# The keys and values of layer 1's memory, computed behind those of layer 0

## The chip, the cores and the metric

The kernel runs on one core of a Trainium2 chip. The metric is device time in microseconds (us), median of several runs. The engines are PE (TensorE: matmuls and transposes, with PEld for its weight loads), DVE (VectorE), ACT (ScalarE), POOL (GpSimd) and SP (SyncE, which issues all DMAs, in order). Each engine carries out its instructions in the order in which the program has them.

## The reference

A trunk of two layers on x (512 x 1024, f32) with a memory of 256 rows. Layer 0 mixes with NSA attention, layer 1 with DSA attention; each layer also has four memory heads, an output projection and a SwiGLU feed-forward network. Cut to what matters here:

```python
for i in range(DEPTH):                                   # 2 layers
    xn = rmsnorm(h, norm_mix[i])
    mix, q_mem = nsa_mixer(xn, nsa_w_in, ...) if i == 0 else dsa_mixer(xn, ...)
    q_mem = q_mem.reshape(B, T, 4, 64) * 64 ** -0.5
    mem_o = memory_attention(q_mem, rmsnorm(mem, norm_mem[i]), w_mem_kv[i])
    h = h + jnp.concatenate([mix, mem_o], axis=-1) @ w_out[i]
    hn = rmsnorm(h, norm_ffn[i])
    h = h + (silu(hn @ ffn_gate[i]) * (hn @ ffn_up[i])) @ ffn_down[i]

def memory_attention(q_mem, mem_n, w_mem_kv):            # mem_n 256 x 1024, w_mem_kv 1024 x 512
    kv = (mem_n @ w_mem_kv).reshape(B, 256, 2, 4, 64)
    k, v = kv[:, :, 0], kv[:, :, 1]
    p = jax.nn.softmax(einsum('bthd,bmhd->bhtm', q_mem, k))
    return einsum('bhtm,bmhd->bthd', p, v)
```

`mem` is an input: its keys and values for layer 1 depend on nothing that layer 0 computes. All attention logits of the mixers get a relative-position bias, which depends on `rel_bias` alone.

## The kernel before

Every f32 product is done as three matmuls of halves: an operand is split into a high part (a cast by ACT) and a low part (the difference, by DVE, or by POOL with `split_ap`). A weight so goes DMA -> `raw` -> `whi` (ACT) -> `wlo` (DVE or POOL) -> PE. `proj_T` takes 128 columns of a weight (512 KB) at a time and has 24 matmuls for them; `proj_tok` takes 4 of the 8 row blocks at a time (512 KB).

A scheduler orders the instructions of each engine by their place in the source, by what they wait for and by when a tile's buffers come free; tiles of one tag share `bufs` buffers.

The start (L855-L878): the two row tiles of mem are loaded, scaled (`scale_row`, L238 on DVE), transposed (`to_T`, L252); `mem_kv` of layer 0 computes keys (`proj_T`, 48 matmuls of 256 columns) and values (`proj_tok`, 48); its four weights use the raw tiles that the projections use too (2 buffers). The four row tiles of x are scaled, both halves by POOL (XSP = (1,1): L235 times rstd, L236 times gain), and transposed. `build_rows` (L353-L377) makes the bias rows: a small matmul (o<-bk,rb, L369), a copy to `row` (L372), a DMA to DRAM `relrow`, and one DMA from `relrow` to `relskew`, which writes for each of 12 heads 128 shifted rows of 512 floats (3 MB). A head's rows come back from there as an M tile (L380, 256 KB, 2 buffers); POOL copies four pieces of each into C (L1038). Then follow the projections of x for layer 0 (nsa weights, matmuls of 512 columns, 24 for a load), the memory's attention (scores s<-kmh,qm at L470, softmax, transposes t<-ident,msb at L425, products), and the heads.

FFN0 (L776, `ffn(0, ...)`) runs eleven units c of gate and up projections with the down projection of the units before in between; FFN1 is the same code for layer 1. In FFN0 at c == 2 `other()` calls `mem_kv1` (L1261): mem is loaded again, its squares are summed again, and `mem_kv(1, ...)` makes the 16 transposes, 48 K matmuls and 48 V matmuls of layer 1's memory. The V weights are split by ACT and POOL (MWK[1] = (0,1)), the K weights by ACT and DVE. Results go to DRAM (`kvd`), from where layer 1 reads them.

## Time and profile before

| | |
|---|---|
| median of 3 runs | 1295.7 us (1294.3 to 1297.49) |
| the profiled execution | 1301.25 us, its span 1299.5 us |
| instructions in the span | 20995 |
| busy | PE 94%, DVE 74%, ACT 52%, POOL 22% |
| DMA | 127.02 MB, mean 98 GB/s |

The span is the stretch between the first and the last instruction in the trace. The page has each engine's busy time, the costliest groups of lines, and the DMA issues. The trace behind it gives, for one engine, a timeline with the idle time before each instruction and what ended it; windows with busy times, granted PE clock and DMA rate; and for a line or a tile its first and last instruction. A matmul's printed duration overlaps the next one's; the step from start to start is what one costs. Regions: the start to some 145 us, layer 0's attention, FFN0 from about 340 to 690 us, layer 1, FFN1 from about 940 to the end.

### The profile page before, as it was taken

The numbers are of one execution on the slowest core, as the hardware profiler recorded it, in microseconds if no ns is written. First come the engines' busy times: TensorE is split into PE (matmuls) and PEld (weight loads), VectorE is DVE, ScalarE is ACT, GpSimd is POOL, SyncE is SP. The second block draws the span as 40 slices with busy tenths as digits, with TensorE's granted clock in tenths as the row PEclk, the third lists the DMA queues.
The fourth block names the chain that finished last, engine by engine and source line by source line (L and its number), as shares of the span: only waits on it lengthen the run. The fifth ranks groups of instructions, "written<-read, shape, count | busy, mean of one in ns | idle before, by whom it ended". The sixth has DMA issues, their size and how long they took to land. (4 is left out here: it accounts for less than half of the span.)

```text
span 1299.5 us, 20995 instructions
## 1 busy us (share of the span) xinstructions
PE 1219.0 (94%) x7810; PEld 1079.4 (83%) x7810; DVE 967.7 (74%) x1763; ACT 672.4 (52%) x1370; POOL 284.6 (22%) x442
## 2 busy tenths in 40 slices
PE   5889999999898999999999778899999999999997
PEld 5668888888888999999998665667799999999995
DVE  6567568998976778777756789948987877777754
ACT  6357376596645444444444365456755444444442
POOL 6440246453301000000004036535420000000001
PEclk9989899999899999999999799999989999999999
DMA  6744221112355333333122010213425333333211
GB/s 228 212 151 118 78 61 51 49 58 71 93 170 180 105 114 98 98 98 111 53 91 81 26 65 29 69 56 110 127 85 154 117 108 107 98 98 98 66 66 65
DMA packets 154842, 127.02 MB, mean 98 GB/s; under 512 B 7240, under 2 KB 129128, under 8 KB 154740
## 3 DMA queue, kind: packets, MB, share of 16 engines
q1 hardware_dynamic: 154740, 125.68, 31.5%
q8 instruction: 61, 1.00, 0.3%
q14 instruction: 41, 0.34, 0.1%
HBM read 122.22 MB, written 6.58 MB: 99 GB/s over the span
## 5 line engine op out<-in xcount | busy, mean ns | idle before, releaser
L245 ACT CAST whi<-rq 128x1024 fp32r<-128x1024 f32 x128 | 134.3, 1051 | 212.2 <-issue 121.7
L246 DVE TENSOR_TENSOR wlo<-rq,whi 128x1024 fp32r<-128x1024 f32 x128 | 159.1, 1251 | 39.9 <-ACT whi L245 39.8
L214 POOL TENSOR_SCALAR ss<-ss 128x1 f32<-128x1 f32 x16 | 7.3, 455 | 627.8 <-ACT sq L212 627.8
L302 PE MATMUL s<-dlo,hh 128*128 128x512 f32 x320 | 125.9, 393 | 1.0 <-DVE dlo L246 1.0
L303 PE MATMUL s<-Xfl,hh 128*128 128x512 f32 x320 | 126.3, 395 | 0.0
L301 PE MATMUL s<-Xfl,hh 128*128 128x512 f32 x320 | 124.4, 394 | 0.0
L554 POOL TENSOR_SCALAR sb<-sb,sm 128x128 f32<-128x128 f32 (+3 forms) x144 | 76.7, 550 | 97.4 <-DVE sm L1384 45.7
L550 ACT ACTIVATE sb<-sb,mx 128x128 f32<-128x128 f32 (+3 forms) x144 | 79.5, 554 | 33.4 <-DVE mx L547 32.7
L688 PE MATMUL X<-Xxl,whi 128*128 128x256 f32 x320 | 89.6, 280 | 0.0
L690 PE MATMUL X<-Xxl,wlo 128*128 128x256 f32 x320 | 89.6, 280 | 0.0
L689 PE MATMUL X<-Xxl,whi 128*128 128x256 f32 x320 | 89.5, 280 | 0.0
L772 DVE TENSOR_TENSOR res<-s,res 128x512 f32<-128x512 f32 x96 | 65.6, 686 | 20.4 <-PE s L303 20.3
L544 DVE CUSTOM_DVE_ANT_0 sb<-s,M 128x512 f32<-128x512 f32 (+3 forms) x144 | 66.2, 482 | 16.6 <-PE s L537 5.6
L303 PEld LDWEIGHTS s<-Xfl,hh 128*128 128x128 f32 x320 | 60.0, 188 | 13.3
L302 PEld LDWEIGHTS s<-dlo,hh 128*128 128x128 f32 x320 | 60.1, 188 | 12.4 <-DVE dlo L246 1.3
L301 PEld LDWEIGHTS s<-Xfl,hh 128*128 128x128 f32 x320 | 60.0, 188 | 11.0 <-DVE res L772 0.3
L245 ACT CAST hh<-c 128x256 fp32r<-128x256 f32 x88 | 35.5, 405 | 56.2 <-DVE c L698 49.5
L689 PEld LDWEIGHTS X<-Xxl,whi 128*128 128x128 f32 x320 | 60.1, 188 | 1.8
L688 PEld LDWEIGHTS X<-Xxl,whi 128*128 128x128 f32 x320 | 60.2, 188 | 1.7
L690 PE MATMUL X<-Xfh,wlo 128*128 128x256 f32 x208 | 59.4, 286 | 2.0 <-DVE wlo L246 2.0
L245 ACT CAST pth<-t 128x512 fp32r<-128x512 f32 (+1 forms) x98 | 48.9, 521 | 23.5 <-PE t L425 20.3
L246 DVE TENSOR_TENSOR ptl<-t,pth 128x512 fp32r<-128x512 f32 (+1 forms) x98 | 57.5, 602 | 4.7 <-ACT pth L245 3.8
(474 smaller groups left out, 4128.7 us busy)
## 6 DMA issues: line engine op xcount, KB each, us to landing
rq<-in_ffn_gate_dram SPq DMA_DIRECT2D x88, 256.0 KB, 2.9
rq<-in_ffn_up_dram SPq DMA_DIRECT2D x88, 256.0 KB, 3.3
draw<-in_ffn_down_dram SPq DMA_DIRECT2D x20, 1024.0 KB, 4.9
M<-relskew SPq DMA_DIRECT2D x36, 256.0 KB, 2.7
raw<-in_w_out_dram SPq DMA_DIRECT2D x16, 512.0 KB, 3.6
raw<-in_nsa_w_in_dram SPq DMA_DIRECT2D x12, 512.0 KB, 4.4
relskew<-relrow SPq DMA_DIRECT2D x1, 3072.0 KB
raw<-in_w_mem_kv_dram SPq DMA_DIRECT2D x4, 512.0 KB, 7.8
```

Source lines behind the costliest of these rows:

```text
L245: act.copy(hi, src)
L246: dve.tensor_sub(lo, src, f(hi))
L301: pe.matmul(o, ah, bh, start=start, stop=False)
L302: pe.matmul(o, ah, bl, start=False, stop=False)
L303: pe.matmul(o, al, bh, start=False, stop=stop)
L544: dve.tensor_tensor_reduce(E[j, br].rearrange("p (k n) -> p k n", n=128), sv[:, :, x, :], Mi.rearrange("p (k n) -> p k n", n=128), 1.0, -3 ...
L550: act.activation(E[j, br], E[j, br], AF.Exp, bias=mx[:, j, br:br + 1], accum_out=sm[:, j, br:br + 1])
L554: pool.tensor_scalar(E[j, br], E[j, br], fc[:, j, br:br + 1], 0.0, op0=OP.mult, op1=OP.add)
L688: pe.matmul(oc, a, xh[:, k], start=first and m == 0 and k == 0, stop=False, skip_group_check=True)
L689: pe.matmul(oc, a, xl[:, k], start=False, stop=False, skip_group_check=True)
L690: pe.matmul(oc, b, xh[:, k], start=False, stop=m == 1 and k == 3, skip_group_check=True)
L772: dve.tensor_add(res[t][:, cs], p, res[t][:, cs])
```

## The change

1. `mem_kv1` is gone from FFN0, with `Two`, `other`, `mt` and `inplace`. Right behind `build_rows` the same `mem_kv(1, ...)` is called with the mem tiles and rstd that layer 0 used; its transposed rows lie in the big tile "fl", the keys in two tiles of the start's pool, the values in the buffer that qs[3] takes later. The results are written to DRAM from there.
2. All weights of `mem_kv` have raw tiles of their own (tag "mraw", 3 buffers).
3. norm_mix's gain has its own tag "gx".
4. XSP = (0,1): the first half of each x row is scaled by one instruction on DVE, the second by POOL as before.
5. In FFN0's tail two tiles are borrowed from other tags.

The diff, without the class `Two`, which is only removed:

```diff
@@ -29,6 +29,7 @@
 WBF = 3
 CHUNK = (2, 5, 3, 4)
 RQ = 6
+MRAW = 3
 WB1 = 2
 EH = 6
 WE = 6
@@ -59,7 +60,7 @@
 QMO = 0
 PT = ("st","t","","fst","o")
 MSP = ((0,0),(0,0))
-XSP = (1,1)
+XSP = (0,1)
 MWK = ((0,0),(0,1))
 PQE = (0,0,1,0,1,1)
 PRE_ = (0,0,0,1)
@@ -189,8 +179,8 @@
     def bcast_rows(src, n, dst):
         dma(dst, bass.AP(tensor=src.tensor, offset=src.offset, ap=[[0, dst.shape[0]], [1, n]]))
 
-    def gain(src, where, bufs=1):
-        g = where.tile([128, D], F32, name=nm("g"), tag="g", bufs=bufs)
+    def gain(src, where, tag="g"):
+        g = where.tile([128, D], F32, name=nm("g"), tag=tag, bufs=1)
         bcast_rows(src, D, g)
         return g
 
@@ -284,7 +274,8 @@
     def wraw(n, where=None):
         assert n <= 1024
         if where is not None:
-            return rq(where)
+            pool_, tag, bufs = where
+            return pool_.tile([128, 1024], F32, name=nm(tag), tag=tag, bufs=bufs)
         return WP["p"].tile([128, 1024], F32, name=nm("raw"), tag="raw", bufs=WP["r"])
 
     def rq(fp, dt=F32):
@@ -380,12 +371,12 @@
         dma(dst, skd[h, :, a:a + n])
 
 
-    def mem_kv(i, xm, rs, wk, kv, mt, f32=False, where=None, inplace=False):
+    def mem_kv(i, xm, rs, wk, kv, mt, f32=False, where=None):
 
         kmh, kml, vm = kv
         g = gain(A["norm_mem"][i], wk)
         for t in range(2):
-            xn = xm[t] if inplace else wk.tile([128, D], F32, name=nm("xn"), tag="xn", bufs=2)
+            xn = wk.tile([128, D], F32, name=nm("xn"), tag="xn", bufs=2)
             scale_row(xm[t], rs[t], g, xn, MSP[i])
             to_T(xn, mt[0], mt[1], t)
         W = A["w_mem_kv"][i]
@@ -782,7 +773,7 @@
             down_mm(t, half, ks, hh, hl, res)
             yield
 
-    def ffn(i, fp, gu0, X, res, fin, early=None, other=None, mt=None):
+    def ffn(i, fp, gu0, X, res, fin, early=None):
         parts = [(0, 1), (1, 3), (3, 5), (5, 7), (7, 9), (9, 11)]
         part_of = {c: pi for pi, (a, b) in enumerate(parts) for c in range(a, b)}
         hs = {}
@@ -793,8 +784,6 @@
                 drain(gu_plain(fp, R, X, *hs[c]))
                 X["sums"]()
                 continue
-            if c == 2 and other:
-                other()
             pi = part_of[c]
             a, b = parts[pi - 1] if pi > 1 else parts[0]
             half = c - parts[pi][0]
@@ -835,7 +824,7 @@
         phase(*PP0)
         W0 = A["nsa_w_in"][0]
         lp = L0.enter_context(_pool(tc, name="l0", bufs=1))
-        qs = {h: lp.tile([128, T], F32R, name=f"qs{h}") for h in range(4)}
+        qs = {h: lp.tile([128, T], F32R, name=f"qs{h}") for h in range(3)}
         mcat = [lp.tile([128, 2, T], F32R, name=f"mcat{x}") for x in range(2)]
         vc4 = lp.tile([128, 2, 4, 128], F32R, name="vc4")
         kcdh = lp.tile([128, 2, 32], F32R, name="kcdh")
@@ -865,8 +854,9 @@
                     rs.append(row_rstd(xm[t], scr))
                 slot = big.tile([128, 4096], F32R, name="mt0", tag="fh")
                 slot = slot.rearrange("p (a k q) -> p a k q", a=2, k=KD)
-                mem_kv(0, xm, rs, sp, kv0, [slot[:, a] for a in range(2)])
-                g = gain(A["norm_mix"][0], sp)
+                mw = (sp, "mraw", MRAW)
+                mem_kv(0, xm, rs, sp, kv0, [slot[:, a] for a in range(2)], where=mw)
+                g = gain(A["norm_mix"][0], sp, "gx")
                 for t in range(NT):
                     dma(res[t], A["x"][0, t * 128:(t + 1) * 128, :])
                 for t in range(NT):
@@ -874,6 +864,16 @@
                     scale_row(res[t], row_rstd(res[t], xn), g, xn, XSP)
                     to_T(xn, xh, xl, t)
                 build_rows(sp)
+
+                kp = [sp.tile([128, NMEM, MEML], F32R, name=f"km1{n}") for n in "ab"]
+                kp.append(lp.tile([128, 2, NMEM, 64], F32, name="vm1", tag="qs3"))
+                slot = big.tile([128, 4096], F32R, name="mt1", tag="fl")
+                slot = slot.rearrange("p (a k q) -> p a k q", a=2, k=KD)
+                mem_kv(1, xm, rs, sp, kp, [slot[:, a] for a in range(2)], True, mw)
+                for d, x in zip(kvd[:2], kp):
+                    dma(d, f(x.rearrange("p a b -> p (a b)")))
+                dma(kvd[2], kp[2].rearrange("p t h d -> p (t h d)"))
+            qs[3] = lp.tile([128, T], F32R, name="qs3", tag="qs3")
             mq = MA.enter_context(_pool(tc, name="mq", bufs=1))
             qm = [mq.tile([128, T], F32R, name=f"qm{h}") for h in range(NMEM)]
             ep = mq
@@ -1147,7 +1147,7 @@
 
         def fin():
             LA["x"] = [big.tile([128, KD, T], F32R, name=f"x1{n}", tag=n) for n in ("xh", "xl")]
-            nl = Lent(ng, dict(xn=(WP["h"], "wlo", 2), sq=(fp, "c12", 1)))
+            nl = Lent(ng, dict(xn=(fp, "hx", 2), sq=(fp, "c12", 1)))
             return norm_to(gain(A["norm_mix"][1], ng), *LA["x"], nl)
 
         def in_proj(fp):
@@ -1225,7 +1225,7 @@
                     if k0 + k < 6:
                         pair = [WP["p"].tile([128, 1024], F32R, name=nm(x), tag=x, bufs=WP["w"]) for x in ("whi", "wlo")]
                     else:
-                        pair = [WP["h"].tile([128, 1024], F32R, name=nm("w3"), tag="whi", bufs=2) for _ in range(2)]
+                        pair = [WP["h"].tile([128, 1024], F32R, name=nm("w3"), tag="raw", bufs=2) for _ in range(2)]
                     pair = [x[:, :912].rearrange("p (k c) -> p k c", c=456) for x in pair]
                     split(raw[:, k:k + 2, :], *pair)
                     ks += [(pair[0][:, j, :], pair[1][:, j, :]) for j in range(2)]
@@ -1258,21 +1258,7 @@
 
             return each
 
-        def mem_kv1():
-
-            kp = [ip.tile([128, NMEM, MEML], F32R, name=f"km1{n}", tag=n) for n in "ab"]
-            kp.append(ip.tile([128, 2, NMEM, 64], F32, name="vm1", tag="c"))
-            xm = [rq(fp) for _ in range(2)]
-            for t in range(2):
-                dma(xm[t], A["mem"][0, t * 128:(t + 1) * 128])
-            rs = [row_rstd(xm[t], fp.tile([128, 1024], F32, name=nm("S"), tag="S", bufs=1)) for t in range(2)]
-            mem_kv(1, xm, rs, ng, kp, mt, True, fp, True)
-            for d, x in zip(kvd[:2], kp):
-                dma(d, f(x.rearrange("p a b -> p (a b)")))
-            dma(kvd[2], kp[2].rearrange("p t h d -> p (t h d)"))
-
-        mt = [Two(*[hslot().rearrange("p (k q) -> p k q", k=4) for _ in range(2)]) for _ in range(2)]
-        ffn(0, fp, gu0, X, res, fin, in_proj, mem_kv1)
+        ffn(0, fp, gu0, X, res, fin, in_proj)
 
 
     with ExitStack() as L1:
```

Since the scheduler sets the order, here is what it made of it. SP's queue from the load of the bias rows on, before (raw_N: nsa weights; relrow, relskew: bias rows):

```order
L297 DMA raw_456<-in_nsa_w_in_dram 128x8x128
L373 DMA relrow<-row 12x640
L297 DMA raw_491<-in_nsa_w_in_dram 128x8x128
L377 DMA relskew<-relrow 1536x1x512
L297 DMA raw_526<-in_nsa_w_in_dram 128x8x128
L297 DMA raw_561<-in_nsa_w_in_dram 128x8x128
L884 DMA posrk<-in_nsa_cmp_pos_k_dram 16x128
L884 DMA posrv<-in_nsa_cmp_pos_v_dram 16x128
```

And after (mraw_N: weights of layer 1's memory, here both halves of the V weights; M_N: bias rows of one head):

```order
L364 DMA relrow<-row 12x640
L368 DMA relskew<-relrow 1536x1x512
L288 DMA mraw_547<-in_w_mem_kv_dram 128x4x256
L288 DMA mraw_553<-in_w_mem_kv_dram 128x4x256
L371 DMA M_1170<-relskew 128x512
L371 DMA M_1176<-relskew 128x512
L371 DMA M_1182<-relskew 128x512
L371 DMA M_1188<-relskew 128x512
L371 DMA M_1380<-relskew 128x512
L371 DMA M_1386<-relskew 128x512
L371 DMA M_1392<-relskew 128x512
L288 DMA raw_707<-in_nsa_w_in_dram 128x8x128
```

Behind relskew stood two loads of nsa weights; now the two V weight loads stand there, then seven M loads, and the third nsa load behind them.

POOL, before, from the last weight split ahead of the first C copies on (w2x: a weight of the compression):

```order
L258 TENSOR_TENSOR w2x_613<-w_76_610,w2x_612 128x256
L1038 TENSOR_SCALAR C<-M_989 128x31
L1038 TENSOR_SCALAR C<-M_989 128x23
L1038 TENSOR_SCALAR C<-M_989 128x15
L1038 TENSOR_SCALAR C<-M_989 128x7
L1038 TENSOR_SCALAR C<-M_995 128x31
L1038 TENSOR_SCALAR C<-M_995 128x23
```

POOL, after, between the two low halves of the V weights (wlo_550 from mraw_547, wlo_556 from mraw_553):

```order
L252 TENSOR_TENSOR wlo_550<-mraw_547,whi_549 128x1024
L1038 TENSOR_SCALAR C<-M_1170 128x31
L1038 TENSOR_SCALAR C<-M_1170 128x23
L1038 TENSOR_SCALAR C<-M_1170 128x15
L1038 TENSOR_SCALAR C<-M_1170 128x7
L1038 TENSOR_SCALAR C<-M_1176 128x31
```

and further on, up to the second of them:

```order
L1038 TENSOR_SCALAR C<-M_1182 128x31
L1038 TENSOR_SCALAR C<-M_1182 128x23
L1038 TENSOR_SCALAR C<-M_1182 128x15
L1038 TENSOR_SCALAR C<-M_1182 128x7
L252 TENSOR_TENSOR wlo_556<-mraw_553,whi_555 128x1024
L1038 TENSOR_SCALAR C<-M_1188 128x31
```

The low halves of the memory's V weights now stand on POOL, with the 12 copies of three M tiles between them.

PE, before, from the last V matmuls of layer 0's memory (f_280) to the first projection of x (f_462):

```order
L302 MATMUL f_280<-wlo_250,mt_126 128x256
L303 MATMUL f_280<-whi_249,mt_126 128x256
L252 MATMUL x_395<-ident,xn_385 128x128 x4
L252 MATMUL x_402<-ident,xn_385 128x128 x4
L301 MATMUL f_462<-xh_98,whi_458 128x512
L302 MATMUL f_462<-xl_99,whi_458 128x512
```

PE, after, in the V matmuls of layer 1's memory, at the first matmul that uses wlo_556 (f_559 and f_585: the two row tiles of mem):

```order
L293 MATMUL f_585<-wlo_550,mt_432 128x256
L294 MATMUL f_585<-whi_549,mt_432 128x256
L293 MATMUL f_559<-wlo_556,mt_432 128x256
L294 MATMUL f_559<-whi_555,mt_432 128x256
L292 MATMUL f_559<-whi_555,mt_432 128x256
```

and the end of these with the first projection (f_678):

```order
L292 MATMUL f_585<-whi_555,mt_432 128x256
L293 MATMUL f_585<-wlo_556,mt_432 128x256
L294 MATMUL f_585<-whi_555,mt_432 128x256
L292 MATMUL f_678<-xh_97,whi_674 128x512
L293 MATMUL f_678<-xl_98,whi_674 128x512
```

The projections of x now stand behind all of layer 1's K and V matmuls. At the memory's attention, before (f_738: a projection, s: scores, t: transposes of softmax rows msb):

```order
L302 MATMUL f_738<-xl_99,whi_734 128x512
L303 MATMUL f_738<-xh_98,wlo_735 128x512
L470 MATMUL s_772<-kmh,qm_440 128x256
L471 MATMUL s_772<-kml,qm_440 128x256
L470 MATMUL s_772<-kmh,qm_441 128x256
L471 MATMUL s_772<-kml,qm_441 128x256
L425 MATMUL t_697<-ident,msb_675 128x128
```

After (f_814: the fifth projection; no other one stands between these scores and their transposes):

```order
L294 MATMUL f_814<-xh_97,wlo_811 128x512
L461 MATMUL s_847<-kmh,qm_619 128x256
L462 MATMUL s_847<-kml,qm_619 128x256
L461 MATMUL s_847<-kmh,qm_620 128x256
L462 MATMUL s_847<-kml,qm_620 128x256
```

and, behind eight more score matmuls like these, PE goes straight to the transposes:

```order
L462 MATMUL s_953<-kml,qm_621 128x256
L461 MATMUL s_953<-kmh,qm_622 128x256
L462 MATMUL s_953<-kml,qm_622 128x256
L416 MATMUL t_878<-ident,msb_856 128x128
L416 MATMUL t_896<-ident,msb_856 128x128
```

Scores of both head pairs now follow the fifth projection directly; the next projection comes some 50 instructions behind the last row shown.

## Rows read from the trace of the kernel before

**Rows 1.** The page, part 1: PE's busy time, share of the span, instructions.

```profile
PE 1219.0 (94%) x7810; PEld 1079.4 (83%) x7810; DVE 967.7 (74%) x1763; ACT 672.4 (52%) x1370; POOL 284.6 (22%) x442
```

**Rows 2.** The answers for single lines of the kernel: L721 from 300 to 740 us (FFN0) and from 900 to 1300 us (FFN1), then L688 from 340 to 760 us and from 940 to 1299 us. Columns: engine, operation, tiles, count: ns of the shortest, median and longest, start in us of the first and of the last.

```profile
L721 ACT COPY c<-X x10: 577/582/598, 361.4 to 649.7; 128x512 f32<-128x512 f32 x10
...
L721 ACT COPY c<-X x10: 575/581/585, 975.4 to 1241.7; 128x512 f32<-128x512 f32 x10
...
L688 PE MATMUL X<-Xxl,whi x160: 277/280/363, 365.2 to 673.6; 128*128 128x256 f32 x160
...
L688 PE MATMUL X<-Xxl,whi x160: 277/280/282, 979.8 to 1265.5; 128*128 128x256 f32 x160
```

**Rows 3.** PE's timeline in FFN0, two neighbouring matmuls of the V projection of layer 1's memory. Columns: start us, duration us, engine, line, operation, output<-inputs, shape, count; in brackets idle time before it and what ended it.

```profile
392.82 0.28 PE L302 MATMUL f<-hh,whi 128*128 128x256 f32 x1
392.94 0.28 PE L303 MATMUL f<-hh,wlo 128*128 128x256 f32 x1
```

**Rows 4.** Groups of instructions by line, PE from 375 to 425 us: the transposes of layer 1's memory rows. Columns after the bar: busy us, mean ns of one, idle us before.

```profile
L252 PE MATMUL x<-ident,rq 128*128 128x128 f32 x16 | 2.2, 272 | 0.0
```

**Rows 5.** Windows around that place. Columns: window in us and its length; busy us and count of PE, PEld, DVE, ACT, POOL; granted PE clock, DMA share, GB/s.

```profile
380.00:390.00 10.00, 8.62 (x54) 7.11 (x53) 9.92 (x16) 5.37 (x11) 0.00 (x0) 1.00 0.62 184
390.00:400.00 10.00, 7.40 (x46) 6.91 (x45) 4.52 (x8) 4.41 (x7) 2.37 (x1) 0.83 0.57 185
400.00:410.00 10.00, 8.03 (x68) 7.82 (x67) 5.90 (x7) 4.24 (x9) 2.38 (x1) 1.00 0.45 145
```

**Rows 6.** PE's timeline at the start: the product of the relative-bias rows, two V matmuls of layer 0 behind a wait, two matmuls of the fourth projection that are two steps apart, the first score of the memory's attention, the first score of the self-attention heads.

```profile
23.51 1.02 PE L369 MATMUL o<-bk,rb 32*12 32x512 f32 x2
...
35.22 0.41 PE L302 MATMUL f<-wlo,mt 128*128 128x256 f32 x1
35.43 0.41 PE L303 MATMUL f<-whi,mt 128*128 128x256 f32 x1
...
62.84 0.39 PE L301 MATMUL f<-xh,whi 128*128 128x512 f32 x1
...
63.31 0.40 PE L303 MATMUL f<-xh,wlo 128*128 128x512 f32 x1
...
71.98 0.28 PE L470 MATMUL s<-kmh,qm 128*128 128x256 f32 x1
...
145.02 0.36 PE L536 MATMUL s<-kd,qs 128*128 128x256 f32 x1
```

**Rows 7.** SP's timeline, the issues of DMAs.

```profile
25.69 0.37 SPq L297 DMA_DIRECT2D raw<-in_nsa_w_in_dram  x1
26.29 0.41 SPq L373 DMA_DIRECT2D relrow<-row  x1
...
30.76 0.89 SPq L377 DMA_DIRECT2D relskew<-relrow  x1
34.02 7.60 SPq L297 DMA_DIRECT2D raw<-in_nsa_w_in_dram  x2
```

**Rows 8.** ACT's timeline, the casts of the two nsa weights of rows 7.

```profile
47.67 1.04 ACT L245 CAST whi<-raw 128x1024 fp32r<-128x1024 f32 x1 [6.90 <-DMA raw<-in_nsa_w_in_dram]
49.39 1.05 ACT L245 CAST whi<-raw 128x1024 fp32r<-128x1024 f32 x1 [0.67 <-DMA raw<-in_nsa_w_in_dram]
```

**Rows 9.** Windows at the start, columns as in rows 5: the time of relskew, and one microsecond of it.

```profile
31.70:45.70 14.00, 11.51 (x60) 9.67 (x61) 8.04 (x12) 4.85 (x10) 6.65 (x7) 0.88 0.83 272
40.00:41.00 1.00, 0.60 (x2) 0.19 (x1) 0.97 (x3) 0.78 (x2) 0.00 (x0) 1.00 0.99 343
```

**Rows 10.** POOL's timeline: gain products of x rows, C copies of one M tile, a subtraction of a weight's high half.

```profile
30.41 2.50 POOL L236 TENSOR_TENSOR xn<-xn,g 128x512 f32<-128x512 f32 x2
...
65.41 0.79 POOL L1038 TENSOR_SCALAR C<-M 128x31 f32<-128x31 f32 x4 [1.97 <-DMA M<-relskew]
...
68.18 2.40 POOL L262 TENSOR_TENSOR wlo<-raw,whi 128x1024 fp32r<-128x1024 f32 x1
```

**Rows 11.** The tile M from 0 to 120 us: its loads on SP's queue (columns as in rows 2), and the time from issue to landing.

```profile
L380 SPq DMA_DIRECT2D M<-relskew x14: 319/320/459, 53.2 to 81.9; - x14
...
DMA to landing us min/median/max: 2.6/3.2/3.9
```

**Rows 12.** The page, part 6: loads of the nsa projection weights; count, KB each, median us from issue to landing.

```profile
raw<-in_nsa_w_in_dram SPq DMA_DIRECT2D x12, 512.0 KB, 4.4
```

**Rows 13.** PE's timeline in the memory's attention: transposes of softmax rows (t<-ident,msb) and score matmuls.

```profile
83.40 0.93 PE L425 MATMUL t<-ident,msb 128*128 128x128 f32 x2 [4.21 <-POOL msb L483]
...
84.77 0.41 PE L471 MATMUL s<-kml,qm 128*128 128x256 f32 x1
...
88.07 0.58 PE L470 MATMUL s<-kmh,qm 128*128 128x256 f32 x1 [0.34 <-ACT msb L479]
...
90.36 0.63 PE L425 MATMUL t<-ident,msb 128*128 128x128 f32 x2
91.43 0.58 PE L470 MATMUL s<-kmh,qm 128*128 128x256 f32 x1 [0.44 <-ACT msb L479]
```

**Rows 14.** VectorE scaling half a row of mem, from 0 to 60 us, columns as in rows 2.

```profile
L238 DVE SCALAR_TENSOR_TENSOR xn<-memx,rstd,g x4: 743/744/751, 8.3 to 10.3; 128x512 f32<-128x512 f32 x4
```

**Rows 15.** VectorE's timeline: the same subtraction of a weight's high half, twice.

```profile
27.08 1.21 DVE L246 TENSOR_TENSOR wlo<-raw,whi 128x1024 fp32r<-128x1024 f32 x1
...
31.63 2.36 DVE L246 TENSOR_TENSOR wlo<-raw,whi 128x1024 fp32r<-128x1024 f32 x1
```

More of the change, by code (lines that the diff above doesn't have):

```diff
@@ L130, in hslot @@
         return where.tile([128, 1024], dt, name=nm("hh"), tag=tag, bufs=2)
-    class Two:
-        def __init__(self, a, b):
-            self.t = a, b
-        def __getitem__(self, at):
-            p, k, n = at
-            if isinstance(k, slice):
-                return self.t[k.start // 4][p, 0:k.stop - k.start, n]
-            return self.t[k // 4][p, k % 4, n]
     class Lent:
```

## The prediction

> **What bounds the kernel now.** I read four views in this order. The page's table of engines first: PE is busy for 94% of the span [rows 1], so a stage is as long as PE's instructions in it, plus what PE waits there. Second, the two feed-forward networks side by side: FFN0 and FFN1 run the same units, and only FFN0 carries the memory's keys and values of layer 1 in it. Third, the windows and PE's timeline around that place, to see what it costs there. Fourth, the queues in the first 75 us, where the work is put now: SP's issues, ACT, POOL, PE. The reader is to see two kinds of time. In FFN0 PE has other matmuls on both sides, so work taken out there is taken off the end. At the start PE doesn't lead; it follows transfers. The prediction is a difference of two numbers of like size.
>
> **Removed from FFN0.** The copy of L721 stands once in each of ten units. From the first to the last it is 649.7 - 361.4 = 288.3 us in FFN0 and 1241.7 - 975.4 = 266.3 us in FFN1 [rows 2]: 22.0 us. The matmuls of X<-Xxl, which end a little later, give 308.4 - 285.7 = 22.7 us [rows 2]. By pieces: 96 matmuls at a step of 392.94 - 392.82 = 0.12 us [rows 3] make 11.5 us, 16 transposes 2.2 us [rows 4], and PE stands idle for 1.38 + 2.60 + 1.97 = 5.95 us in the three windows around them [rows 5], since its clock fell to 0.83 in one of them and the weights came late. That is 19.7 us, without what the lower clock cost. I take 22.0, with 19.7 and 22.7 as ends. The second load of mem, its squares and the second gain load go with it; they lay beside PE. The tiles that the tail of FFN0 borrows instead (an xn from "hx", a weight pair from "raw") come free behind the same readers as those of before; I cost them at nothing, and the cover is FFN1's form of the same code, which has them so already.
>
> **Added at the start: PE's own work.** 16 transposes and 96 matmuls, 2.2 + 11.5 = 13.7 us at full clock. If PE were the limit there, this would be the price. It isn't.
>
> **Added at the start: the wait.** In the order that the scheduler wrote, I follow the last half of the V weights, wlo_556.
>
> 1. relskew starts as before. The row product o<-bk ran at 23.51 [rows 6]; now 12 matmuls (1.4 us) and 8 transposes (1.3 us) more stand ahead of it, so about 26.2. relrow followed 2.8 us later, at 26.29 [rows 7], with another subtraction ahead of its copy on VectorE, which now stands elsewhere; I take 1.8 us, thus 28.0, and keep the 1.0 us for the range. relskew, which waits for relrow, was issued 4.5 us after it, at 30.76 [rows 7], and a 512 KB load had gone out just ahead of relrow, at 25.69, which is 1.7 us by step 2, where none goes now. So relskew goes at 28.0 + 4.5 - 1.7 = 30.8, as before.
> 2. Behind relskew in the queue before were two nsa loads, issued from 34.02 on [rows 7]. ACT waited 6.90 us for the first and began at 47.67, then 49.39 for the second [rows 8]: 1.72 us for 512 KB, so relskew itself was through at about 47.67 - 1.72 = 45.9. In these 14 us the queues moved 272 GB/s, up to 343 in one microsecond [rows 9]. The V weights of layer 1 stand in that very place now: they land at 47.6 and 49.4.
> 3. ACT's cast of the first takes 1.04 [rows 8], POOL's subtraction 2.40 [rows 10]: wlo_550 is ready at 51.1.
> 4. Here POOL's order decides. Between wlo_550 and wlo_556 it has 12 C copies of three M tiles, 0.79 us for each four [rows 10]. M has two buffers. M 1 and 2 can only be issued when relskew is complete (45.9), land behind the V weights at 50.3 and 51.2, and are copied by 51.9 and 52.7. M 3 needs the buffer of M 1: issued 51.9, landed 3.2 us later, the median of an M load [rows 11], 55.1, copied 55.9, and wlo_556 is ready at 55.9 + 2.4 = 58.3.
> 5. PE stands at wlo_556 with 26 V matmuls left. 13 of them at the half-clock step of 35.43 - 35.22 = 0.21 us [rows 6] (PE has been waiting) and 13 at 0.12 make 4.3: 62.6. Then five projections of 24 matmuls at (63.31 - 62.84) / 2 = 0.235 us [rows 6], 28.1: PE begins the memory's scores at 90.7. Before, it did at 71.98 [rows 6]. The loss is 18.7 us.
>
> What could be late in those 28 us: the third nsa load (raw_707) now stands behind seven M loads, and PE needs it second. 14 M loads went out from 53.2 to 81.9 before [rows 11], 2.2 us each; with the 2.4 us of wlo_556 in POOL's way the seventh goes at about 60, raw_707 lands 4.4 us after its issue [rows 12], 64.8, is split by 67.1, and is needed at 62.6 + 5.6 = 68.2. It holds, by about 1 us. The own tag "mraw" lets two nsa loads go early; what they gain is behind the V matmuls and so worth nothing.
>
> **Moved: the memory's attention.** Before, a whole projection stood behind the first scores, and PE still waited 4.21 us at 83.40 for POOL, then 0.34 and 0.44 [rows 13]: 5.0 us. Now the scores come with no projection behind them. A softmax takes from the end of the scores of 84.77 to their transposes at 90.36, 5.4 us [rows 13]. The first such wait has eight more score matmuls (0.9 us) as cover and costs 4.5; the second has 20 instructions (2.9 us) and costs 2.5. The projection is only moved, so 7.0 - 5.0 = 2.0 us are added. The ends: 5.0 us gained, if POOL, done with its C copies by then, is never late; 11.2 lost, as the slow rival has it.
>
> **XSP.** A half row on POOL takes a product with rstd and one with the gain, the latter 1.25 us (2.50 for two [rows 10]); on VectorE it is one instruction of 0.743 us [rows 14]. Four halves moved make POOL's x rows over 4 x 1.25 = 5 us shorter. With PE waiting to 58.3 that is worth nothing in the sum; if that wait were gone, up to those 5 us.
> What the trace shows against it: VectorE's subtraction of 128x1024 took 1.21 us at 27.08, alone, and 2.36 us at 31.63 [rows 15], while POOL's gain products ran from 30.41 to 32.91 [rows 10]. The Trainium skill, "SBUF — State Buffer", section "SBUF: two separate sides", says that VectorE with two SBUF inputs and a GpSimd operation that reads SBUF lock each other out entirely for a whole instruction. The trace agrees with that rule. Two half rows on VectorE, each held up for a POOL product of 1.25 us ahead of the row copy, would make relrow, and all of steps 1 to 5, up to 2.5 us later. I take nothing, since the row copy waits for PE until 26 anyway.
>
> **Sum.** -22.0 + 18.7 + 2.0 = -1.3 us. The profiled execution took 1301.25 us, 5.55 over the median of 1295.7; it would become 1299.95, and a median 1294.4.
>
> **Rivals.**
> - *relskew alone is faster.* Before, it shared the queues with nsa loads; now nothing goes with it. Its 3.15 MB at 343 GB/s take 9.2 us and at 272 GB/s 11.6 [rows 9], against the 15 from 30.76 to 45.9: with 4 us less, and M loads at their 2.6 us [rows 11], 4.6 us less in step 5. Then -22.0 + 14.1 + 2.0 = -5.9: 1289.8. For it: the share of the DMA engines is not full over the whole stretch. Against it: the loads behind it waited until it was through, so that they hardly took part.
> - *Slower: the softmax chains stand bare.* Place: PE from the first scores to the next projection. Price: three chains of 5.4 us in full are 16.2, less the 5.0 of before, 11.2 us instead of 2.0, and the net +7.9: 1303.6. It decides from the point where these waits come to over 10.2 us (then the time is more than 3.9 us above before). For it: the order has scores, transposes and products there and nothing long; the clock could fall in it, as it had at 88.07, where a score matmul shows 0.58 us [rows 13] and not the 0.28 of 71.98 [rows 6]. Against it: POOL has no C copies left by then, and the second halves of the heads overlap the first.
> - *The lock on VectorE* delays relskew by 2.5 us: 1296.9.
> - *The change doesn't do what it says:* FFN0 keeps its length, because what PE waited for there is the weight stream. Then +20.7. FFN1 shows that the same units run 22 us shorter without it [rows 2], so I give it no chance of its own.
>
> **How the numbers follow.** A measurement of this kernel tells 0.3%, 3.9 us, from no change. Forecast 0.48 (1289 to 1299: faster 0.15, same 0.26, slower 0.07). A faster relskew 0.26 (faster 0.22, same 0.04). Bare softmax chains 0.17 (slower 0.16, same 0.01). The lock 0.09 (faster 0.02, same 0.04, slower 0.03). Together faster 0.39, same 0.35, slower 0.26. The range goes from 1283, where the faster relskew meets the 5.0 us of POOL's waits gone, to 1303, just under the slow rival; about a tenth is left out on each side.
>
> **What would show it.** Right: L721's first to last in FFN0 within 2 us of FFN1's; ACT's V casts at about 47.7 and 49.4; PE with a wait of several us for POOL's wlo of the V weights, ending near 58; the first memory score near 91. Wrong: PE without such a wait (then the start costs 13.7 us or less and the time is below 1288), V weights that land before 45, or a first head that comes more than 24 us later than at 145.02 [rows 6].

## The result and the profile after

The changed kernel takes 1305.93 us (median of 4 runs, 1305.23 to 1306.46) against 1295.0 for the kernel before in the same comparison: 1.0084 times, 95% interval [1.0065, 1.0102]. It is 10.9 us slower, and 2.9 us beyond the end of the forecast range; the forecast was 1294.4.

The page after, its first lines:

```profile
span 1303.9 us, 20980 instructions
...
PE 1218.3 (93%) x7810; PEld 1081.7 (83%) x7810; DVE 971.4 (75%) x1767; ACT 671.4 (51%) x1366; POOL 275.4 (21%) x430
```

PE is as busy as in [rows 1] (1218.3 against 1219.0 us); the span is 4.4 us longer than the 1299.5 of before. That is not the 10.9 us of the medians: the profiled execution of before was a long one (1301.25 against a median of 1295.7), that of after lies on its median (1305.85). A second trace of before (e1 below) spans 1294.2 us. The stages, each from the start of one instruction to the start of another (us):

| stage | before | e1: before again | after |
|---|---|---|---|
| start to first memory score | 72.0 | 71.1 | 97.7 |
| to the first score of the heads | 73.0 | 70.2 | 69.8 |
| to the first copy (L721, now L712) in FFN0 | 216.4 | 214.8 | 220.0 |
| FFN0, first to last such copy | 288.3 | 288.8 | 265.9 |
| to the first in FFN1 | 325.7 | 325.3 | 326.5 |
| FFN1, first to last | 266.3 | 266.3 | 266.0 |
| to the end | 57.8 | 57.7 | 58.0 |

Against e1: +26.6 at the start, -0.4, +5.2 in the heads, -22.9 in FFN0, +1.2 in layer 1, 0.0 behind: 9.7 us.

The copy that answers to [rows 2], in FFN0 and FFN1:

```profile
L712 ACT COPY c<-X x10: 573/581/587, 387.5 to 653.4; 128x512 f32<-128x512 f32 x10
...
L712 ACT COPY c<-X x10: 573/580/589, 979.9 to 1245.9; 128x512 f32<-128x512 f32 x10
```

Both stretches are now 266 us. SP's issues, which answer to [rows 7]:

```profile
27.14 0.37 SPq L364 DMA_DIRECT2D relrow<-row  x1
29.59 0.88 SPq L368 DMA_DIRECT2D relskew<-relrow  x1
32.34 3.70 SPq L288 DMA_DIRECT2D mraw<-in_w_mem_kv_dram  x2
45.56 14.80 SPq L371 DMA_DIRECT2D M<-relskew  x7
60.46 0.38 SPq L288 DMA_DIRECT2D raw<-in_nsa_w_in_dram  x1
...
69.82 0.80 SPq L288 DMA_DIRECT2D raw<-in_nsa_w_in_dram  x1
70.67 1.70 SPq L884 DMA_DIRECT2D posrk<-in_nsa_cmp_pos_k_dram  x1
```

relskew went out at 29.59; behind it the V weights, seven M loads, the third nsa weight (60.46), and, last of what PE needs here, the positions (70.67). ACT's casts, which answer to [rows 8] (the V weights, then the third nsa weight):

```profile
47.04 1.04 ACT L251 CAST whi<-mraw 128x1024 fp32r<-128x1024 f32 x1 [2.98 <-DMA mraw<-in_w_mem_kv_dram]
50.32 1.05 ACT L251 CAST whi<-mraw 128x1024 fp32r<-128x1024 f32 x1 [2.23 <-PE f L293]
...
65.68 1.05 ACT L235 CAST whi<-raw 128x1024 fp32r<-128x1024 f32 x1 [1.93 <-DMA raw<-in_nsa_w_in_dram]
```

POOL from the first low half of the V weights to the second:

```profile
48.16 2.39 POOL L252 TENSOR_TENSOR wlo<-mraw,whi 128x1024 fp32r<-128x1024 f32 x1 [13.60 <-ACT whi L251]
50.52 1.56 POOL L1038 TENSOR_SCALAR C<-M 128x31 f32<-128x31 f32 x8
54.45 1.74 POOL L1038 TENSOR_SCALAR C<-M 128x31 f32<-128x31 f32 x4 [2.38 <-DMA M<-relskew]
56.16 2.34 POOL L252 TENSOR_TENSOR wlo<-mraw,whi 128x1024 fp32r<-128x1024 f32 x1
```

And PE, which answers to [rows 6]:

```profile
58.56 0.39 PE L293 MATMUL f<-wlo,mt 128*128 128x256 f32 x1 [2.79 <-POOL wlo L252]
...
63.13 0.53 PE L292 MATMUL f<-xh,whi 128*128 128x512 f32 x1
...
77.70 0.28 PE L886 MATMUL t<-ident,posrk 16*128 16x16 f32 x1 [3.02 <-DMA posrk<-in_nsa_cmp_pos_k_dram]
...
78.10 0.80 PE L292 MATMUL f<-xh,whi 128*128 128x512 f32 x1
...
97.68 0.28 PE L461 MATMUL s<-kmh,qm 128*128 128x256 f32 x1
...
102.14 0.58 PE L461 MATMUL s<-kmh,qm 128*128 128x256 f32 x1 [3.34 <-ACT msb L470]
```

PE waited 2.79 us for POOL at 58.56, was through with V at 63.13, then waited 3.02 us for posrk (the positions) at 77.70. The matmul behind that wait shows 0.80 us, not 0.40. The clock was granted at 0.84 on average from 60 to 92 us, and at 0.50 (1.2 of 2.4 GHz) behind the wait, up to 83.9:

```profile
60.00:92.00 32.00, 28.98 (x115) 23.57 (x114) 11.53 (x16) 9.61 (x15) 13.29 (x34) 0.84 0.70 207
...
77.10:83.90 6.80, 6.20 (x16) 4.90 (x17) 3.10 (x5) 2.23 (x3) 3.12 (x4) 0.50 0.31 78
```

From 77.70 to 97.68 there are 72 matmuls of 512 columns, 16.9 us at the step of [rows 6]; they took 20.0.

In the heads PE waits where it did not before. The view of waits, from the first head to FFN0 (us in total, times, longest). VectorE adds a product to the rows (res) or scales queries (qs), and PE needs the buffer that it reads the product from:

```profile
PE f L292 <- DVE res L593: 4.0, 3, 1.6
...
PE f L292 <- DVE qs L330: 2.2, 2, 1.2
```

In e1 neither of the two is among PE's waits of that stretch; what is left there (3.6 us for rows scaled by VectorE and less) is in both. The scheduler wrote the heads in another order: of PE's first 1000 instructions from the first head on, 696 stand in the order of before. The change touches no line of their code; qs[3] alone has another buffer.

### The profile page after: what moved, and what is told of

Same layout as the page of the kernel before. It is cut to its first block, busy times and chain, and to the rows that moved or that the text cites. A ratio compares the mean times of both kernels' runs of the same rounds, so it can differ in the third digit from the quotient of the medians.

```text
span 1303.9 us, 20980 instructions
## 1 busy us (share of the span) xinstructions
PE 1218.3 (93%) x7810; PEld 1081.7 (83%) x7810; DVE 971.4 (75%) x1767; ACT 671.4 (51%) x1366; POOL 275.4 (21%) x430
## 5 line engine op out<-in xcount | busy, mean ns | idle before, releaser
L236 DVE TENSOR_TENSOR wlo<-rq,whi 128x1024 fp32r<-128x1024 f32 x126 | 155.3, 1240 | 30.3 <-ACT whi L235 30.2
L293 PEld LDWEIGHTS s<-dlo,hh 128*128 128x128 f32 x320 | 60.1, 188 | 11.0
L680 PEld LDWEIGHTS X<-Xxl,whi 128*128 128x128 f32 x320 | 60.1, 188 | 1.9
L236 DVE TENSOR_TENSOR ptl<-t,pth 128x512 fp32r<-128x512 f32 (+1 forms) x98 | 57.7, 602 | 4.1 <-ACT pth L235 3.2
L679 PE MATMUL X<-Xfh,whi 128*128 128x256 f32 x208 | 59.8, 289 | 0.9 <-ACT Xfh L235 0.9
L680 PE MATMUL X<-Xfh,whi 128*128 128x256 f32 x208 | 59.9, 288 | 0.6 <-DVE Xfh L236 0.6
```

What stands on the lines that cost most here:

```text
L236: dve.tensor_sub(lo, src, f(hi))
L293: pe.matmul(o, ah, bl, start=False, stop=False)
L679: pe.matmul(oc, a, xh[:, k], start=first and m == 0 and k == 0, stop=False, skip_group_check=True)
L680: pe.matmul(oc, a, xl[:, k], start=False, stop=False, skip_group_check=True)
```

## The experiments

Each timed run has the kernel before beside it on the same chip (medians 1295.8 to 1297.0).

**A second trace of before, and the two waits at the start.**

> The kernel before, unchanged, for a second trace. Theory: the profiled execution of before (1301.25 us) was a long one of its kind, 5.5 us over the median, and the change's true loss is the 10.9 us of the medians; then this trace spans some 1293 to 1295 us, and its stretches show where the 5 to 6 us were: in the start up to the first memory score (71.98), in the 73.0 us to the first head, in the 149.2 us of the heads, or in FFN0. Rival: the profile itself costs before 5 us and the changed kernel none; then this trace spans 1299 us again, with a time near 1301.

1296.44 us (1291.69 to 1300.14); ratio 1.0002 [0.9987, 1.0018], span 1294.2. The first head and FFN0:

```profile
L536 PE MATMUL s<-kd,qs x72: 276/394/525, 141.3 to 288.9; 128*128 128x512 f32 x36, 128*128 128x384 f32 x24, 128*128 128x256 f32 x12
...
L721 ACT COPY c<-X x10: 577/580/597, 356.1 to 644.9; 128x512 f32<-128x512 f32 x10
```

Against the first trace 3.7 us are in the stretch up to the first head (141.3 against 145.0) and 1.6 in that to FFN0. The profile doesn't cost 5 us; one execution was long.

e2 loads the positions early (the edit, cut; the two loads further down, which go, are not shown):

```diff
                     dma(res[t], A["x"][0, t * 128:(t + 1) * 128, :])
+                posr = [mp.tile([16, 128], F32, name=f"posr{s}") for s in "kv"]
+                for s, pr in zip("kv", posr):
+                    dma(pr, A[f"nsa_cmp_pos_{s}"][0].rearrange("(j a) d -> j (a d)", a=2))
```

> The changed kernel with the two position loads (posrk, posrv) issued right behind x, and nothing else changed. Theory: PE stood 3.02 us at the transpose of posrk (77.70) because its load was behind the fifth nsa weight and eleven M loads on SP, and then ran 24 matmuls and more at half clock; from 77.70 to the first score it took 19.98 us for 72 matmuls that take 16.9 at full clock. So 3.0 + 3.1 = 6.1 us go: 1299.8 median, first score at 91.6 (97.68 in the changed kernel). Rival: the next load of the same queue takes its place (the fourth or fifth nsa weight); then PE waits there and at most 2 us go: over 1303.5.

e3 splits the V weights with VectorE, e4 does both:

```diff
-MWK = ((0,0),(0,1))
+MWK = ((0,0),(0,0))
```

> The changed kernel with the low halves of layer 1's V weights on VectorE in place of POOL (MWK[1] = (0,0)). Theory of the prediction (POOL's place between the C copies decides): PE's wait of 2.79 us at 58.56 goes, and the half clock behind it (26 matmuls at 0.21 instead of 0.12, 2.4 us): V ends near 58 instead of 63.1, and the time falls by up to 5 us, to 1301. Rival: what is late is the position load behind the nsa weights and M loads on SP, whose place doesn't depend on POOL's split; then PE only waits longer there and the time stays within 1.5 us of 1305.9.

> Both edits together: position loads early, V split by VectorE. If the two waits are all that the start costs over PE's own work, the first score comes at 97.68 - 6.1 - 5 = 86.6 and the time is 1294.8, the kernel before's 1295.0 within 0.3%. Rival: with both waits gone the nsa weights behind the M loads (third to fifth) are what PE waits for, and the first score stays over 89, the time over 1297.

1305.35 (1.0074 times before, [1.0058, 1.0089]), 1305.52 (1.0076, [1.0060, 1.0092]) and 1305.15 us (1.0070, [1.0053, 1.0088]): nothing won by any. e3 went as its rival has it; PE's wait for POOL is gone and that for the positions is there, a little longer than in the changed kernel (3.02):

```profile
78.05 0.23 PE L886 MATMUL t<-ident,posrk 16*128 16x16 f32 x1 [3.42 <-DMA posrk<-in_nsa_cmp_pos_k_dram]
```

e2 and e4 did move the first memory score, from 97.7 to 90.6 and 88.5, but the first head only from 167.5 to 165.9 and 164.6. In e4, PE at the memory's attention:

```profile
88.54 0.28 PE L461 MATMUL s<-kmh,qm 128*128 128x256 f32 x1
...
98.53 0.58 PE L461 MATMUL s<-kmh,qm 128*128 128x256 f32 x1 [5.73 <-ACT msb L470]
```

The softmax chain stands bare: 5.73 us for ACT's msb, 3.34 in the changed kernel. Between the two rows PE also waited 2.49 us, at 91.43, for queries (qm) that ACT and VectorE scale. ACT had stood idle just before:

```profile
85.90 1.05 ACT L251 CAST whi<-raw 128x1024 fp32r<-128x1024 f32 x1 [2.97 <-DMA raw<-in_nsa_w_in_dram]
```

That is the sixth nsa weight, issued at 81.82, no sooner than in the changed kernel (81.10): the next load of the same queue was late in their place. In this stage the clock was granted at 0.50 for 17.1 us, against 10.2 in the changed kernel. And the stretch of the heads took 221.5 and 221.8 us. The two waits are true ones, and their removal was worth nothing in the time.

**The work in neither place, and the other edits alone.** e5 leaves out `mem_kv(1, ...)` and writes layer 0's keys and rows of mem where its results went; e8 is the kernel before with XSP, MRAW and "gx" and without the move.

> The changed kernel with the keys and values of layer 1's memory computed nowhere: their place in DRAM is filled with the keys of layer 0 and with rows of mem, so layer 1's memory attention has other numbers and the same instructions. It prices the work in either place. By the traces, taking it out of FFN0 is worth 22.9 us (288.8 against 265.9 between L721's first and last copy), so this kernel takes 1295.8 - 22.9 = 1273 us; the changed kernel then pays 1305.9 - 1273 = 33 us for the work at the start. Theory: 5 of these 33 are in the heads (first head to FFN0: 220.0 us in the changed kernel, 214.8 in the one before), whose order of instructions on PE differs only because of the move; here the order is that of before and the stretch takes 215 us. Rival: the heads are slower for another edit (XSP, the raw tiles), then the stretch takes 220 us here too and the time is 1278.

> The kernel before with the other edits and without the move: XSP = (0,1), raw tiles of their own for layer 0's memory weights, a tag of its own for norm_mix's gain; layer 1's memory stays in FFN0. Theory: the whole loss belongs to the move, and these edits take 0 to 3 us off the start, since the x rows come sooner: 1293 to 1296. Rival: the nsa weights, loaded sooner, stand in the way of the weights of layer 0's memory (DMA share 0.97 in the first 30 us of the changed kernel, 0.76 before), and these edits alone cost 3 us or more: over 1299.

e5 takes 1286.72 us, 14 more than expected. FFN0 has its 265.9 and the stretch of the heads 217.4 (215 expected; one wait of 1.6 us for res is left); the first head comes at 143.1. But layer 1 takes 334.0 us, 8.7 more than in e1, and its order of instructions on PE is another one too. So the time without the work is no clean price; the stages are: the work costs 24.4 us at the start (167.5 - 143.1) and 22.9 in FFN0. e8: 1296.53, ratio 0.9995 [0.9983, 1.0007], first head 143.2, stretch of the heads 214.9. These edits alone lose nothing.

**The order of the heads.** e6 changes one number, so that POOL scales the second half of the rows of layer 1's memory:

```diff
-MSP = ((0,0),(0,0))
+MSP = ((0,0),(0,1))
```

> The changed kernel with one small edit at the start: the second half of each row of layer 1's memory is scaled by POOL, not VectorE (MSP[1] = (0,1)). By it the scheduler writes the heads in the order of before again (999 of their 1000 first instructions on PE stand in that order, against 696 in the changed kernel); the start keeps its waits. Theory: the order costs 5.2 us, so the stretch from the first head to FFN0 takes 215 us and the time is 1300.7. Rival: the stretch is longer because of what the heads get late (bias rows, weights), not because of the order: 220 us again, and a time within 2 us of 1305.9.

1301.4 us (1.0037 times before, [1.0023, 1.0050]), first head 166.0, first head to FFN0 212.8:

```profile
L527 PE MATMUL s<-kd,qs x72: 276/393/501, 166.0 to 311.6; 128*128 128x512 f32 x36, 128*128 128x384 f32 x24, 128*128 128x256 f32 x12
```

The heads proper take 145.6 us here and 152.6 in the changed kernel:

```profile
L527 PE MATMUL s<-kd,qs x72: 277/394/501, 167.5 to 320.1; 128*128 128x512 f32 x36, 128*128 128x384 f32 x24, 128*128 128x256 f32 x12
```

Of the 7.2 us won in the whole stretch (212.8 against 220.0), layer 1 lost 4.1 (330.6 against 326.5). Its order changed too; that this is the reason is not shown, since e14, with the same order there, takes 328.5. The counter-test puts the changed kernel's order into a kernel without the move. e13 is e8 with one edit:

```diff
-MWK = ((0,0),(0,1))
+MWK = ((0,1),(0,1))
```

> The kernel of e8 (before, with the edits of XSP, raw tiles and gain tag, without the move; 1296.5 us, first head to FFN0 214.9) with one edit more: the low halves of layer 0's V weights on POOL. By it the heads on PE come out in the changed kernel's order, while layer 1's memory stays in FFN0. Theory: the order costs the heads 5 to 7 us, so first head to FFN0 takes 220 to 222 us, and the time is near 1301 unless the start gains from the edit. Rival: the heads are long because of the move (buffers of qs[3], bias rows loaded earlier): 213 to 217 us here.

1309.24 us (1.0098, [1.0084, 1.0112]), 12.7 more than e8 and 8 more than expected. First head to FFN0 is 222.6 us (214.9 in e8), and the heads' scores and PE's waits are:

```profile
L540 PE MATMUL s<-kd,qs x72: 277/394/658, 144.5 to 299.3; 128*128 128x512 f32 x36, 128*128 128x384 f32 x24, 128*128 128x256 f32 x12
```

```profile
PE f L305 <- DVE res L606: 4.1, 3, 1.6
...
PE f L305 <- DVE qs L343: 1.4, 2, 1.2
```

The same waits, of nearly the same length, without the move. In the ten traces with the order of before (two of them of before itself) the stretch is 212.7 to 217.4 us, in the seven with the other 219.8 to 222.6. The waits for res and qs come to 5.4 to 6.2 us in each of the seven; of the ten, only e5 and e7 have any of them, 1.6 us. Nor is it what e6's edit does by itself: e9 and e14 (below) differ in that edit alone, and there it goes with the long stretch, 220.6 against 214.5. The order is the cause. Where the clock was granted at 0.50 for equally long in the stretch (6.8 us in the changed kernel and e6, 13.7 in e13 and e8), the order makes 7.2 and 7.7 us; e1 has 13.7 us of it, so the changed kernel's 5.2 against e1 probably understate it. The other 3.6 us between e13's and e8's traces are the start (1.3) and layer 1 (2.2).

**Other places at the start.** e7 puts layer 1's memory ahead of `build_rows`, e10 ahead of the x rows (with e6's edit too), e12 `build_rows` ahead of the x rows (scaled by VectorE).

> The changed kernel with layer 1's memory ahead of build_rows in place of behind it. SP then issues the V weights and all five nsa weights ahead of relrow and relskew, POOL has no C copies between the V weights' low halves, and the heads come in the order of before. Theory: of the 33 us that the work costs at the start 13.7 are PE's own, 5.2 the heads' order, and the rest waits and low clock behind relskew (3 MB ahead of the V weights). With relskew behind them the first memory score comes near 71.1 + 13.7 + 2 = 87 and the heads take 215: 1295.8 - 22.9 + 16 = 1289, faster than before. Rival: relskew, now some 15 to 20 us later, makes the bias rows (C, M) late for the first heads; then what is won at the start is lost there, and the time is over 1297.

> Layer 1's memory directly behind layer 0's, ahead of the x rows (and the second halves of its rows scaled by POOL); heads and layer 1 come out in the order of before (0.999 and 0.997). relskew goes out behind the nsa weights. Theory: PE works through both memories while x lands, but the bias rows come 15 us later, and as in e7 (82.6 us from the first memory score to the first head) that is paid there: first head 164 to 171, time 1295 to 1302. Rival: with PE never waiting for V weights behind relskew the start costs PE's own 13.7 us only: first head 157, time 1288.

> The changed kernel with build_rows ahead of the x rows, and the x rows scaled by VectorE alone; heads and layer 1 in the order of before (0.996 and 0.997). Theory: relrow still waits for PE's matmul and the queue in front of it, relskew goes a few us sooner, the V weights behind it too; first head 161 to 166, FFN0 266, time 1293 to 1299. Rival: VectorE, which now has the x rows too, makes the row copy and the splits late: first head at 168 or more, time over 1301.

1307.52 (1.0082, [1.0066, 1.0098]), 1301.32 (1.0042, [1.0027, 1.0056]) and 1299.35 us (1.0022, [1.0008, 1.0035]). e7 has the first memory score at 87.9, as forecast, and the first head at 170.5. What it pays in between shows first in a softmax chain with nothing beside it, not in late bias rows for the heads, as the rival had it. ACT, and VectorE behind it, stood for a weight of the compression, which was loaded behind relskew (issued at 73.65 and 72.74):

```profile
90.75 1.04 ACT L235 CAST whi<-raw 128x1024 fp32r<-128x1024 f32 x1 [5.31 <-DMA raw<-in_nsa_cmp_k_w_dram]
```

```profile
87.90 0.28 PE L461 MATMUL s<-kmh,qm 128*128 128x256 f32 x1
...
97.34 0.58 PE L461 MATMUL s<-kmh,qm 128*128 128x256 f32 x1 [8.33 <-ACT msb L470]
```

e10 and e12 have the heads' short order (212.7 both) and a first head at 169.0 and 166.1.

**XSP, and POOL's order.** e11 undoes XSP.

> The changed kernel with both halves of the x rows scaled by POOL again (XSP = (1,1)). The prediction gave this edit no worth in the sum, since PE waited for the V weights anyway. Theory: the same time within 1.5 us (1304.5 to 1307.5), and PE's wait for the second low half of the V weights (2.79 us in the changed kernel) gone or shorter, since K comes later. Rival: PE's chain over the x rows and the rows of layer 1's memory leads at the start, so 3 us or more are lost: over 1309.

1305.68 us (1.0066, [1.0048, 1.0084]), the same as the changed kernel; but PE's wait got longer, against what was expected. The first low half came sooner here (39.84 us against 48.16, its load ahead of relskew), the second later (59.87 against 56.16), since relskew went out at 32.23 and sixteen C copies stand between the two:

```profile
62.26 0.58 PE L293 MATMUL f<-wlo,mt 128*128 128x256 f32 x1 [8.69 <-POOL wlo L252]
```

e9 has e6's edit and e13's in the changed kernel; e14 only e13's; e15 joins e9's two, e2's and XSP = (1,1).

> The changed kernel with two small edits at the start (low halves of layer 0's V weights on POOL too, second halves of layer 1's memory rows scaled by POOL), by which both the heads of layer 0 and layer 1 come out in the order of the kernel before (0.999 and 0.997 of PE's instructions). Theory: the time is then that of before plus the start minus FFN0 and nothing else: heads 215 us from first head to FFN0, layer 1 325 us, first head at 166 to 169 against 141 to 143, FFN0 266: 1295.8 + 25 - 22.9 = 1298, so 5 to 8 us under the changed kernel and still 1 to 4 over before. Rival: layer 1 was long in e6 (330.6) for data that come late, not for its order; then it is 329 to 331 here too and the time is 1302.

> The changed kernel with only the low halves of layer 0's V weights on POOL; the heads come out in the order of before, layer 1 in that of e6. In e9 POOL had 4 C copies between the two low halves of layer 1's V weights where the changed kernel has 12; the second one ended at 54.3 instead of 58.5 and the posrk load went out at 64.2 instead of 70.7. Theory of the prediction's step 4: POOL's order is what made the start long; if the copies between are few here too, the first head comes at 158 to 161 us, heads 213 to 215, layer 1 329 to 331, time 1294 to 1297. Rival: e9's start came from the memory rows that POOL scaled (second halves): first head 165 or later here, time over 1299.

> The changed kernel with e9's two edits, position loads early and the x rows scaled by POOL; heads, layer 1 and FFN1 come out in the order of before. Theory: start as in e9 (first head 157 to 160), heads 213 to 215, FFN0 266, layer 1 326: 1288 to 1292, faster than before by 4 us or more; the move then pays FFN0's 22.9 us with 16 to 18 at the start. Rival: with the x rows on POOL the second low half of the V weights is late again (e11: PE waited 8.7 us for it) and the first head comes at 164 or later: 1296 or more, no better than before.

e9: 1297.92 us (1.0012, [1.0000, 1.0024]). Its premise was wrong: the heads of the kernel that ran stand in the changed kernel's order (220.6 us); it won its 8 us at the start, first head 158.9. e14: 1295.31 us (1292.63 to 1297.76), 0.9996 of before [0.9984, 1.0008]. On POOL the second low half stands behind eight C copies, not twelve, with no wait for the third M tile, and starts 4 us sooner (52.19 against 56.16):

```profile
48.06 2.40 POOL L252 TENSOR_TENSOR wlo<-mraw,whi 128x1024 fp32r<-128x1024 f32 x1 [10.25 <-ACT whi L251]
50.43 1.55 POOL L1038 TENSOR_SCALAR C<-M 128x31 f32<-128x31 f32 x8
52.19 2.39 POOL L252 TENSOR_TENSOR wlo<-mraw,whi 128x1024 fp32r<-128x1024 f32 x1 [0.20 <-ACT whi L251]
```

The positions are issued earlier too,

```profile
64.80 0.87 SPq L884 DMA_DIRECT2D posrk<-in_nsa_cmp_pos_k_dram  x1
```

PE passes both places with waits of 0.4 us at most, ends V at 58.6 (63.1 in the changed kernel), has the first memory score at 87.8 and the first head at 159.2. POOL's order alone doesn't make this: e6 has the second low half as soon, behind eight copies,

```profile
52.52 2.39 POOL L252 TENSOR_TENSOR wlo<-mraw,whi 128x1024 fp32r<-128x1024 f32 x1 [0.22 <-ACT whi L251]
```

and V's end at 60.1, but then PE waits 2.4 us for ACT and 1.7 us for the positions among the projections, and the first head comes at 166.0. In e14 the heads have the short order (214.5 us to FFN0):

```profile
L527 PE MATMUL s<-kd,qs x72: 276/394/628, 159.2 to 306.3; 128*128 128x512 f32 x36, 128*128 128x384 f32 x24, 128*128 128x256 f32 x12
```

Layer 1 has e6's order and 328.5 us. e15, 1295.43 us (1.0003, [0.9991, 1.0016]), not the 1288 to 1292 expected: first head 162.9 (the wlo starts at 57.07 again), stretch of the heads 215.5, layer 1 328.2. Neither is faster than before. Against e1, e14 pays 17.9 us up to the first head and 3.2 in layer 1, and gets 22.5 in FFN0 and 0.3 in the heads: 1.7 us, which the medians don't tell from nothing.

## Why the prediction was wrong, by its steps

- **FFN0, -22.0.** Right: -22.4 in the traces it was made from, -22.9 against e1.
- **Steps 1 to 5 up to the end of V.** Right, size and mechanism: relskew 30.8 forecast and 29.6 measured, wlo_556 ready 58.3 and 58.5, V's end 62.6 and 63.1. e6 and e14 show the mechanism: with eight copies in between and not twelve, POOL's second low half starts some 4 us sooner and V ends at 60.1 and 58.6. One detail was turned round, without harm to the sum: the half clock lay on the second half of those 26 matmuls (from 60.0 us), not on the first.
- **"What could be late in those 28 us": the first step that failed.** I followed the third nsa weight, which came in time (cast at 65.68), and stopped there. The positions stood ten issues further down the same queue, and PE's transposes of them are in its order between the second projection and the third. They cost 3.0 us, and the low clock behind them 3.1: five projections took 34.6 us, not 28.1, and the first memory score, the sign of the prediction that failed, came at 97.7, not near 91. It was a chain and not one item: with the positions early (e2) the memory's attention grew by 5.5 us and the first head came only 1.6 sooner. Price the whole queue behind an added wait, not the next item.
- **The memory's attention, +2.0.** Too much: 69.8 us against 70.2 in e1, so -0.4 (against the 73.0 of [rows 6], in the long execution, -3.2). Of the two chain waits that I priced at 7.0 us PE had 3.34 at the first; none stood at the second, but 2.2 us in three waits of 0.9 at most at the last transposes (131 to 134 us). The first does grow where PE comes early: 5.73 us in e4, 8.33 in e7.
- **The heads: a term that was not there, the second step that failed.** +3.6 in the traces it was made from and +5.2 against e1. I compared the orders up to the memory's attention, where the code had changed, and took the rest as moved whole. e6 and e13 show that the order alone makes 7 to 8 us.
- **XSP, worth nothing.** Right (e11), though PE's wait with it was shorter.
- **The sum.** In the traces: +7.0 at the start, -5.2, +3.6, -0.4, +0.7 behind, with the forecast of -1.3: +4.4. Against e1 the misses are +7.9 (start), -2.4 (memory's attention), +5.2 (heads), -0.9 (FFN0) and +1.2 (layer 1), which make +9.7 of -1.3. The start and the heads are thus what failed. The other 6.5 us of the 10.9 are the step from the profiled execution to the median. I wrote the difference of the two down and then took the change off both. But the 5.3 us by which that execution was long (e1) lay in the start and the heads, in the very stages from which I took terms.
- **The rivals.** None was it. "Relskew alone is faster" is refuted: from its issue to the cast of the weight behind it are 17.5 us here (29.59 to 47.04) and 16.9 before (30.76 to 47.67). The lock on VectorE is there (below), but cost relrow nothing. The slow rival had the right form and the wrong place; its point of decision was summed wrong, too, since waits of 12.2 us, not 10.2, make the time 3.9 us longer (-8.3 and the waits). No rival was "the scheduler rewrites code that I didn't touch".

Open stays why the scheduler writes one order or the other, what the start costs by each item of the queue (SP's order changes with POOL's: four M loads stand ahead of the third nsa weight in e14, seven in the changed kernel, nine in e3 and e4), and how much of the loss is due to layer 1's order in a kernel where all else is as in e14.

## What to carry to other kernels

Where a scheduler orders the whole program, compare the orders over the whole program before and after, and price each stage in which they differ: an edit at the start moved 5 to 8 us in a stage that begins some 100 us later. Moving work from a stage that PE leads (13.7 us of PE there cost 22.9, with its waits) to one that a queue leads is worth only what the queue behind it allows; follow every item behind the added wait that PE, or an engine that it waits for, needs. And take a difference of stages only from executions that lie on the median; a single profile was 5 us long in the stages that counted.

## What the runs showed that I had not expected

How the lock that the prediction weighed looks in the rows. VectorE's scaling of half an x row, and POOL's product with rstd that meets it:

```profile
21.38 0.75 DVE L228 SCALAR_TENSOR_TENSOR xn<-res,rstd,g 128x512 f32<-128x512 f32 x1 [2.74 <-POOL rstd L192]
...
28.35 1.11 DVE L228 SCALAR_TENSOR_TENSOR xn<-res,rstd,g 128x512 f32<-128x512 f32 x1
```

```profile
21.45 1.24 POOL L225 TENSOR_SCALAR xn<-res,rstd 128x512 f32<-128x512 f32 x1
...
28.23 0.69 POOL L225 TENSOR_SCALAR xn<-res,rstd 128x512 f32<-128x512 f32 x1
```

At 21.38 VectorE is first and takes 0.75 us; POOL's product, begun at 21.45, takes 1.24, which takes 0.69 where it is first, at 28.23. There VectorE is second, at 28.35, and takes 1.11. So the second of two is longer by 0.55 and 0.36 us, where the first still had 0.68 and 0.57 to do. The Trainium skill, "SBUF — State Buffer", section "SBUF: two separate sides", has the later of a VectorE operation with two SBUF inputs and a GpSimd operation that reads SBUF wait until the earlier is done; the trace agrees with that to within 0.2 us. The prediction bounded the price too high, at 2.5 us: relrow went out at 27.14, 0.9 before the 28.0 forecast, and VectorE was first at both x rows that stand ahead of the row copy. The subtraction at 27.08 that the prediction calls alone met a POOL instruction on 128x1 as well, which began at 27.44 and took 0.90 us (0.19 at 17.03 in the changed kernel), until VectorE was done.
